# Three engines put on a written order of issue, from the output projection to the end of the first feed-forward loop

## The chip, the core and the metric

The kernel runs on one NeuronCore of one Trainium2 chip. The core has a matrix engine (TensorE, PE in the profile), a vector engine (VectorE, DVE), a scalar engine (ScalarE, ACT), GpSimd (POOL) and SyncE (SP), which here issues loads. Each of these works through its own instruction stream in order, and they wait for one another by semaphores. Tiles lie in SBUF (128 partitions); the sums of TensorE go to PSUM, which has eight banks of 128 x 512 floats. The metric is the device time of one execution in microseconds: 1062.6 us for the kernel before, the median of three runs (1062.28 to 1067.63).

## What is computed

One transformer-like block on 512 tokens of width 1024, all in float32, depth 1. Cut to what matters:

```python
h = rms_norm(x, mix_pre_g)
proj = h @ w_in                                   # convolution branch, state-space branch, gates
mixed = (g_conv * conv_out + g_ssm * ssm_out) @ w_out
x = x + rms_norm(mixed, mix_post_g)
h = rms_norm(x, ffn_pre_g)
gt, up = jnp.split(h @ w_gate_up, 2, axis=-1)     # hidden width 2816
f = (jax.nn.silu(gt) * up) @ w_down
x = x + rms_norm(f, ffn_post_g)
```

The change lies between `@ w_out` and the end of `h @ w_gate_up`. What stands before and after it in the program is not edited.

## The kernel before

**Precision.** Every float32 product is made of three faster ones: each operand is split into a rounded part (`...h`, `hi`) and the remainder (`...l`, `lo`), and `mm3` (lines 182 to 186) issues high x high, low x high and high x low into one PSUM sum. So every weight piece of 128 x 1024 has to be split: a copy on ScalarE (line 140 or 860) makes the high part, a subtraction on VectorE (line 145 or 863) the low part.

**Loads.** `w_raw` (line 133) loads the pieces on SyncE's queue, in the order of the program, into five buffers called `raw`. A buffer is loaded again when the last reader of what it held is done. Pieces 105 to 112 are the eight of W_out, 113 to 116 the first of each of the feed-forward slices 0 to 3, 117 to 120 the second of each of these, 121 and on the rest.

**Output projection (lines 1039 to 1057 and 1088 to 1126).** The 512 tokens are four tiles `t` of 128; each has two sums `tm_wo_t_n` of 512 columns, so eight banks, with eight steps `k` of contraction: 24 matmuls for each sum, `wo_step`. As soon as a token tile is summed, `residual(t)` makes of it the new residual stream: squares on ScalarE (`jk_a`), the product with the gain on VectorE (`mg`), a factor by GpSimd (`pm_a`, `rs_a`), the sum with x (`xr`), again squares (`jk_b`) and a factor (`pm_b`, `rs_b`), and a diagonal matrix `dg` of that factor. `turned(t)` multiplies by this diagonal on TensorE, which transposes and normalises at once (`ptr`), `gained` multiplies by the gain (`xg`: one half on VectorE, one on ScalarE).

**Feed forward, first product (lines 1059 to 1308).** It is done by a seven-product scheme (Winograd's form of Strassen's) for each of 22 slices `u` of weights. The moving operands are seven forms of the normalised tokens: `b11`, `b21`, `b22`, `t1` to `t4`; the first half of each comes from token tiles 0 and 1, the second from tiles 2 and 3, so most are complete only when all four tiles are through (`late_forms(3)`). The weight forms are `a11/a12` (from the first piece), `s1`, `s3/a22` and `s2/s4` (four additions of 128 x 512 on VectorE, line 888, then three splits). The products go to two banks for each slice, `xy` and `v`: `x1`, `y1`, `x2`, `v1`, `x3`, `v2`, `x4`, of 12 matmuls each with 256 columns. Between them halves of the banks are copied out (ScalarE, lines 1196, 1205, 1213) or added out (VectorE, line 1184): `x2` may not write into its bank before `x1_out` and `y1_out` have read it. The copies go to tiles `sg` and `f32`, whose memory lies where the pools of the residual and the late forms lay (closed in lines 1173 and 1174).

**What sets the order.** The Tile framework schedules the traced program at compile time with its own costs, and each engine's stream is the result. `pin(last, engines)` (line 171) takes the instructions of an engine after `last` in the order of the program and adds an edge from each to the next. Such an edge is an order within one stream, and no semaphore. In the kernel before, lines 1058 to 1167 (from `square_a(1, 0)` to `first(4)`) are pinned on the three engines, and so is the loop of slices 5 to 21 (lines 1278 to 1308); the first part (lines 1039 to 1057) and the loop of slices 0 to 4 (lines 1169 to 1277) are left to the scheduler.

Of the kernel before, what the change touches and what calls it, by code (L numbers as in the profile page):

```python
# [17 lines left out]
PE_Q, ACT_Q, DVE_Q = [getattr(mybir.EngineType, n) for n in ("PE", "Activation", "DVE")]  # L18
# [89 lines left out]
ORDER += [(_b, _j) for _b in BLOCKS for _j in range(NQ)]  # L108


def b3(ap, n):

    return ap.unsqueeze(len(ap.shape)).to_broadcast(list(ap.shape) + [n])
# [3 lines left out]
def block_kernel(ctx: ExitStack, tc: tile.TileContext, x, xT, prm, hp, gp, w, out):  # L117
    nc = tc.nc
# [28 lines left out]
    def w_split(n, pool_=None, tags=None, bufs=2, parts=1):  # L147
        if n in split or n >= W_END:
            return
        for r in range(n, n + RAW_AHEAD):  # L150
            w_raw(r)
        tags, bufs = (tags, bufs) if tags else (("whi", "wlo"), W_BUFS)
        split[n] = [(pool_ or wp).tile([P, 1024], F32R, tag=tg, bufs=bufs, name=f"{tg}_{n}") for tg in tags]
        if parts == 1:
            w_part(n, slice(0, 1024))
# [15 lines left out]
    def pin(last, *engines):  # L171

        traced = nc.cur_bb.bb.instructions
        at = next(n for n in reversed(range(len(traced))) if traced[n] is last)
        edge = mybir.DependencyInfo(mybir.DependencyClass.NoSync, mybir.DependencyReason.DATA)
        for e in engines:
            row = [i for i in traced[at + 1 :] if i.engine == e]
            for one, two in zip(row, row[1:]):
                tc.add_manual_dep(two, one.name, edge, reason="order")
        return traced[-1]  # L180
# [272 lines left out]
    for j in range(NK):  # L453
# [11 lines left out]
        if j == 0:  # L465
# [7 lines left out]
            first = pv, pg  # L473
# [54 lines left out]
    def s1(g):  # L528
# [5 lines left out]
        for c2 in range(2):  # L534
            ps = aux_tile(f"pxT{g}_{c2}")
            for c in range(2):
                tok = slice((2 * c2 + c) * P, (2 * c2 + c + 1) * P)
                for e in range(2):
                    pe.transpose(ps[:, c * GW + e * P : c * GW + (e + 1) * P], s[f"x{e}"][:, tok], ident)
            cs = slice(2 * c2, 2 * c2 + 2)  # L540
            pv = ps.rearrange("p (c h d) -> p c h d", c=2, h=HG)
            dve.tensor_tensor(out=xdt[:, cs], in0=pv, in1=b3(dtt[:, cs, hs], HD), op=ALU.mult)
            dve.tensor_tensor(
                out=y[:, cs], in0=pv,
                in1=b3(hp_t[:, 2:3, hs].to_broadcast([P, 2, HG]), HD), op=ALU.mult,
            )
        dve.tensor_tensor(out=xdec, in0=xdt[:, : NT - 1], in1=b3(dec[:, : NT - 1, hs], HD), op=ALU.mult)
        ps = yd_tile(0, f"pBT{g}")
        for c in range(NT - 1):
# [329 lines left out]
    def steps_s(u):  # L879

        if u >= NF or (u, "s1") in forms:
            return [], [], [], [], []
        ra, rb_ = g_raw(u, 0), g_raw(u, 1)
        (a11, a12), (a21, a22) = [(r[:, :T], r[:, T:]) for r in (ra, rb_)]
        s1_ = w2.tile([P, T], F32, tag="s1", bufs=2, name=f"s1_{u}")

        def total(out_, one, two):
            return lambda: dve.tensor_tensor(out=out_, in0=one, in1=two, op=ALU.add)  # L888

        return (  # L890
            [total(s1_, a21, a22), total(a21, a11, a21)],
            [total(a11, s1_, a11), total(a12, a11, a12)],
            halve(("s1",), u, s1_, [w2.tile([P, T], F32R, tag=tg, bufs=2, name=f"{tg}_{u}") for tg in ("dhi", "dlo")]),
            halve(("s3", "a22"), u, rb_, pair_of_tiles()),
            halve(("s2", "s4"), u, ra, pair_of_tiles()),
        )
# [125 lines left out]
    def late_forms(t):  # L1022
# [13 lines left out]
            ("t1", t1, 1.0), ("t2", t2, -1.0), ("t3", t1, 1.0), ("t4", t2, 1.0), ("b22", x1, 1.0))}  # L1036
        return s, {n: v[0] for n, v in h.items()}, {n: v[1] for n, v in h.items()}

    for k in range(2, NK):
        w_split(wo0 + k, *((wp, ("whi", "wlo")) if k > 5 else (w2, ("chi", "clo"))), W_BUFS if k > 5 else 3)  # L1040
    ps = tm_tiles("wo")
# [15 lines left out]
    here = nc.cur_bb.bb.instructions[-1]  # L1057
# [14 lines left out]
    def first(u):  # L1072
        x1(u)
        y1(u)
# [70 lines left out]
    one, two, s1, s3, s2 = steps_s(0)  # L1145
# [19 lines left out]
    hi["t3"]()  # L1165
    lo["t3"]()
    first(4)
    pin(here, PE_Q, ACT_Q, DVE_Q)
    s["t4"]()
    for n in ("b22", "t4"):  # L1170
        hi[n]()
# [105 lines left out]
    here = nc.cur_bb.bb.instructions[-1]  # L1277
    for u in range(EARLY_U + 1, NF):
# [7 lines left out]
        one, two, s1, s3, s2 = steps_s(u + 1)  # L1286
# [73 lines left out]
    def f_form(n):  # L1360
        p, j = jobs[n]
        q = j // 2
        if (p, q) in f_forms:
            return
        if p == "d":
            hi, lo = [t.rearrange("p (k t) -> p k t", k=2) for t in f_room(n)]
            src, sign = f32[:, 2 * q : 2 * q + 2, :], 1.0
        else:
            hi, lo = [t.rearrange("p (k t) -> p k t", k=4) for t in f_room(n)]
            ka, kb = slice(4 * q, 4 * q + 4), slice(NPAIR + 4 * q, NPAIR + 4 * q + 4)  # L1370
            a11, a12, a21, a22 = f32[:, ka, c1], f32[:, kb, c1], f32[:, ka, c2], f32[:, kb, c2]
            s = room["s"][:, ka] if room else None
            if p == "p5":
                dve.tensor_tensor(out=s, in0=a22, in1=a21, op=ALU.subtract)
            elif p == "p6":
                dve.tensor_tensor(out=a21, in0=a11, in1=a21, op=ALU.add)
                dve.tensor_tensor(out=s, in0=a21, in1=a22, op=ALU.subtract)
            elif p == "p3":
                dve.tensor_tensor(out=s, in0=a12, in1=s, op=ALU.subtract)
            src = {"p1": a11, "p5": s, "p6": s, "p3": s, "p7": a21, "p2": a12, "p4": a22}[p]  # L1380
            sign = -1.0 if p in ("p1", "p7") else 1.0
        f_forms[p, q] = hi, lo
        act.activation(hi, src, AF.Copy, scale=sign)
        if sign > 0:
            dve.tensor_tensor(out=lo, in0=src, in1=hi.bitcast(F32), op=ALU.subtract)
        else:
            dve.scalar_tensor_tensor(out=lo, in0=src, scalar=-1.0, in1=hi.bitcast(F32), op0=ALU.mult, op1=ALU.subtract)

    here = pin(here, PE_Q, ACT_Q, DVE_Q)
    f_form(0)  # L1390
    for j in range(2):
        w_form(j)
# [5 lines left out]
    x4(NF - 1)  # L1398
    last_out(NF - 1)
    pin(here, PE_Q)  # L1400
    h2.close()
    pf = ctx.enter_context(tc.tile_pool(name="pf", bufs=1))
# [70 lines left out]
    for t in range(NT):  # L1473
        i, r = t % 2, t // 2
# [99 lines left out]
```

## Time and profile before

| what | value |
|---|---|
| median of three runs | 1062.6 us |
| the profiled execution, its own time | 1061.24 us |
| its span, first to last instruction | 1059.5 us |
| TensorE busy | 1040.6 us (98%) |
| VectorE busy | 826.2 us (78%) |
| ScalarE busy | 599.0 us (57%) |
| GpSimd busy | 93.4 us (9%) |
| mean granted TensorE clock | 0.994 |

A row of the view of stretches gives for each engine the microseconds busy in the stretch and, in brackets, how many instructions began in it; then the granted clock of TensorE (1.00 is full) and the DMA engines' share. A row of the timeline gives the start, the duration, the engine, the line, the operation, output and inputs, and in square brackets how long the engine had been idle and what released it. Matmuls overlap in that view: their cost is the distance from start to start. A row of the view of waits says who waited for whom: microseconds in total, times, the longest.

### The profile page before, as it was taken

To read this page: it belongs to the slowest core of one execution; us is meant where nothing else is said; L and a number is where in the kernel's file an instruction comes from. 1 tells how busy PE (TensorE), PEld (TensorE's weight loads), DVE (VectorE), ACT (ScalarE), POOL (GpSimd) and SP (SyncE) were. 2 spreads that over 40 slices of the span, in tenths; PEclk is the share of its full clock that TensorE was granted. 3 is DMA by queue.
4 is the path that set the end of the run, shared out by engine and by line. 5 is a ranking of instruction groups with operands and counts; after the bars stand their busy time and mean duration, and the time that the engine had idled before them with its cause. 6 is when DMAs were issued, how large, how long until landed. Compare 5 with 4: busy or idle time off the path is not lost.

```text
span 1059.5 us, 15639 instructions
## 1 busy us (share of the span) xinstructions
PE 1040.6 (98%) x6145; PEld 920.5 (87%) x6145; DVE 826.2 (78%) x1178; ACT 599.0 (57%) x970; POOL 93.4 (9%) x117
## 2 busy tenths in 40 slices
PE   8999999999999999999999999998999999999997
PEld 7888789888989898989888888888999999998886
DVE  7799897886589769787996545458998898879765
ACT  6657847594849373933332593266555555555641
POOL 2002001111101020100000100011000000022001
PEclk9999999999999999999999999999899999999999
DMA  7477563656544645362123313524443334168912
GB/s 278 131 182 218 141 142 96 179 127 167 125 125 111 182 105 154 103 156 61 60 80 123 97 45 134 179 83 117 134 125 121 120 101 162 58 122 182 296 37 80
DMA packets 39098, 138.75 MB, mean 131 GB/s; under 512 B 4592, under 2 KB 4848, under 8 KB 38000
## 3 DMA queue, kind: packets, MB, share of 16 engines
q1 hardware_dynamic: 27168, 93.12, 26.8%
q0 software_dynamic: 8352, 33.56, 15.9%
q10 hardware_dynamic: 3504, 11.08, 2.9%
q8 instruction: 48, 0.79, 0.3%
q14 instruction: 26, 0.21, 0.1%
HBM read 133.48 MB, written 4.26 MB: 130 GB/s over the span
## 4 chain that ended last, share of the span: by engine, by line
PE 78%; DVE 12%; ACT 6%; issue 2%; DMA 1%; POOL 0%; SPq 0%; DVEq 0%; POOLq 0%; ACTq 0%
DVE a L417 4%; PE xy L184 3%; PE xy L185 3%; PE xy L186 3%; PE yd L579 3%; PE pso L184 2%; PE pso L185 2%; PE v L184 2%; PE pso L186 2%; PE v L185 2%; PE v L186 2%; PE px L184 2%; PE px L185 2%; PE px L186 2%; PE sx L186 2%
## 5 line engine op out<-in xcount | busy, mean ns | idle before, releaser
L140 ACT CAST whi<-raw 128x1024 fp32r<-128x1024 f32 (+1 forms) x118 | 120.9, 1033 | 223.4 <-PE pC L185 43.4
L417 DVE SCALAR_TENSOR_TENSOR a<-v,prm_t,a 128x485 f32<-128x485 f32 (+17 forms) x240 | 179.7, 753 | 4.5 <-ACT a L414 0.9
L145 DVE TENSOR_TENSOR wlo<-raw,whi 128x1024 fp32r<-128x1024 f32 (+1 forms) x84 | 99.8, 1195 | 43.8 <-ACT whi L140 43.6
L184 PE MATMUL pz<-whi,hhi 128*128 128x256 f32 (+1 forms) x256 | 74.2, 290 | 0.0
L185 PE MATMUL pz<-wlo,hhi 128*128 128x256 f32 (+1 forms) x256 | 73.2, 286 | 0.0
L186 PE MATMUL pz<-whi,hlo 128*128 128x256 f32 (+1 forms) x256 | 72.8, 284 | 0.0
L143 POOL DMA_DIRECT2D wlo<-in_w x34 | 30.3, 891 | 257.3 <-ACT wlo L142 169.4
L184 PE MATMUL pso<-yh,whi 128*128 128x512 f32 x128 | 50.0, 393 | 0.0
L184 PE MATMUL px<-hhi,whi 128*128 128x512 f32 x128 | 49.9, 390 | 0.0
L185 PE MATMUL px<-hlo,whi 128*128 128x512 f32 x128 | 49.9, 390 | 0.0
L185 PE MATMUL pso<-yl,whi 128*128 128x512 f32 x128 | 49.9, 391 | 0.0
L186 PE MATMUL px<-hhi,wlo 128*128 128x512 f32 x128 | 49.8, 389 | 0.0
L186 PE MATMUL pso<-yh,wlo 128*128 128x512 f32 x128 | 49.8, 392 | 0.0
L185 PEld LDWEIGHTS pz<-wlo,hhi 128*128 128x128 f32 x256 | 49.0, 191 | 0.3
L184 PEld LDWEIGHTS pz<-whi,hhi 128*128 128x128 f32 x256 | 49.0, 191 | 0.2
L186 PEld LDWEIGHTS pz<-whi,hlo 128*128 128x128 f32 x256 | 49.0, 191 | 0.1
L863 DVE TENSOR_TENSOR wlo_g<-raw,whi_g 128x1024 fp32r<-128x1024 f32 x39 | 47.4, 1220 | 1.7 <-ACT whi_g L860 1.2
L860 ACT CAST whi_g<-raw 128x1024 fp32r<-128x1024 f32 x39 | 40.8, 1053 | 13.2 <-DVE raw L888 13.2
L400 ACT ACTIVATE L<-L,nacs 128x128 f32<-128x128 f32 x128 | 41.3, 392 | 1.9 <-POOL L L394 1.6
L494 DVE SCALAR_TENSOR_TENSOR x<-px,prm_t,x 128x511 f32<-128x511 f32 (+2 forms) x48 | 35.6, 743 | 1.5 <-ACT x L492 1.3
L142 ACT ACTIVATE wlo<-whi 128x1024 fp32r<-128x1024 f32 x34 | 35.9, 1056 | 0.2
L860 ACT CAST chi_g<-raw 128x1024 fp32r<-128x1024 f32 x24 | 25.1, 1055 | 13.3 <-DVE raw L888 11.1
(531 smaller groups left out, 3359.6 us busy)
## 6 DMA issues: line engine op xcount, KB each, us to landing
raw<-in_w SPq DMA_DIRECT2D x161, 512.0 KB, 3.7
wlo<-in_w POOLq DMA_DIRECT2D x34, 512.0 KB, 6.0
L<-scr POOLq DMA_DIRECT2D x8, 1024.0 KB, 5.4
raw_p<-in_w ACTq DMA_DIRECT2D x8, 512.0 KB, 7.8
chain<-in_w POOLq DMA_DIRECT2D x6, 512.0 KB, 6.2
xT<-in_xT SPq DMA_DIRECT2D x8, 256.0 KB, 5.5
xr<-in_x ACTq DMA_DIRECT2D x4, 512.0 KB, 5.4
x2d<-xr ACTq DMA_DIRECT2D x4, 512.0 KB, 2.8
```

The lines of the kernel that those rows point to most:

```text
L140: act.copy(hi[:, c], src[:, c])
L142: act.activation(lo[:, c], hi[:, c].bitcast(F32), AF.Copy, scale=-1.0)
L145: dve.tensor_tensor(out=lo[:, c], in0=src[:, c], in1=hi[:, c].bitcast(F32), op=ALU.subtract)
L184: mark["pe"] = pe.matmul(ps, lh, rh, start=start, stop=False, skip_group_check=more)
L185: pe.matmul(ps, lh, rl, start=False, stop=False, skip_group_check=more)
L186: pe.matmul(ps, ll, rh, start=False, stop=stop, skip_group_check=more)
L400: act.activation(L[:, h, c, :], L[:, h, c, :], AF.Exp, bias=nacs[:, c, HG * g + h : HG * g + h + 1])
L417: return dve.scalar_tensor_tensor(out=va[j][:, d:], in0=vs[j][:, : T - d], scalar=col("dw_w", j * KC + KC - 1 - d), in1=va[j][:, d:], op0= ...
L494: dve.scalar_tensor_tensor(out=a[:, d:], in0=ps[:, : T - d], scalar=col("ssm_w", i * KS + KS - 1 - d), in1=a[:, d:], op0=ALU.mult, op1=ALU ...
L579: pe.matmul(yd[c // 2][:, c % 2, h, :], s["L"][:, h, c, :], s["xdt"][:, c, h, :], start=True, stop=True)
L860: act.copy(hi, src)
L863: dve.tensor_tensor(out=lo, in0=src, in1=hi.bitcast(F32), op=ALU.subtract)
```

## The change

A table `ISSUE` gives, for TensorE, ScalarE and VectorE, a list of numbers. Number n is the n-th instruction (from 0) of that engine in program order, counted from the first instruction after `before_wo`, which is set just before line 1039, the splits of W_out's pieces. `listed` takes the engine's instructions from there to line 1389, puts them in the order of the list, and adds an edge from each to the next, as `pin` does. Both calls of `pin` for this part go; the last `pin(here, PE_Q)` of line 1400 stays and starts where the list ends. No instruction is added, dropped or altered, DMA issues on ScalarE's queue included (they are numbered like the others). SyncE and GpSimd get no list.

The lists have 2036 numbers for TensorE, 248 for ScalarE and 327 for VectorE. From 815, 128 and 154 on they are the order of the program, which is that of `pin` before; ahead of these they are a new order. Some of the numbers, counted out by the code:

- TensorE: 0 to 95 `tm_wo` of token tiles 0 and 2, 108-115 `ptr0`, 140-147 `ptr2`, 196-203 `ptr1`, 160-195 and 204-215 `tm_wo` of tile 3, 216-239 slice 0's `x1` and `y1`, 288-295 `ptr3`, 344-355 slice 0's `x2`, 356-367, 416-427 and 476-487 `v1` of slices 0, 1 and 2, 404-415 slice 1's `x2`, 536-547 `v1` of slice 3.
- VectorE: 51 to 54 the four additions of slice 0, 61 `dlo` (the low part of `s1`) of slice 0, 59 `clo_g11` and 64 `wlo_g10` (the low parts of slice 0's `s2/s4` and `s3/a22`), 33 and 48 the low parts of `a11/a12` of slices 2 and 3, 31 `dg1`, 49 `dg3`, 62 `t1l`, 68 and 65 `t4l` and `t3l` of token tiles 2 and 3, 73 `clo_g13`, 93 `dlo` of slice 3, 116 `wlo_g22`.
- ScalarE: 64 `dhi` of slice 0, 58 `chi_g11`, 66 `whi_g10`, 73 the first copy out of `xy`, 81 the last read of slice 0's `xy`.

```diff
--- before.py
+++ after.py
@@ -108,6 +108,28 @@
 ORDER += [(_b, _j) for _b in BLOCKS for _j in range(NQ)]
 
 
+ISSUE = (
+    (PE_Q,
+     "0-75 78-80 84-86 90-92 76-77 81-83 87-89 93-95 99-101 105-107 119-121 125-127 108-115 96-98 102-104 116-118 "
+     "122-124 128-130 134-136 148-150 154-156 131-133 137-139 151-153 157-159 140-143 184-195 160-171 144-147 196-203 "
+     "172-183 204-215 264-275 296-307 216-239 308-319 276-295 320-331 240-263 356-367 332-343 416-427 476-487 344-355 "
+     "380-391 404-415 368-379 440-451 428-439 392-403 464-475 500-511 452-463 536-547 488-499 524-535 512-523 548-559 "
+     "596-607 584-595 560-571 620-643 608-619 572-583 656-667 644-655 704-715 692-703 668-691 716-739 752-775 800-811 "
+     "740-751 776-787 812-814 788-799 815-2035 "),
+    (ACT_Q,
+     "0-3 5 4 11 6-9 12 10 13-14 64 16-18 15 29 19-20 22 30 21 31-35 41 49 58 37 66 42 36 38 43 27 44-46 39-40 48 50 "
+     "23-26 28 71 53-56 51 57 52 47 59-62 68 65 70 63 77 69 67 73 97 88 72 82 75 90 84 74 76 78 83 79 86 92 85 89 81 "
+     "87 104 93 98 80 91 99-100 94 103 95 105 108 96 101 106-107 102 109 112 110-111 114 118 116 119 117 115 120-121 "
+     "123 125 122 113 127 124 126 128-247 "),
+    (DVE_Q,
+     "0-4 6-7 5 8-9 51-52 10 13 12 11 14 16 15 21 17 61 19 25 18 20 26-29 53 22 30 54 31 33 48 59 34 64 35 23 36-37 32 "
+     "69 40-41 39 42 44 24 45 70 74 47 43 46 49 71 50 38 56 55 57 72 58 62 78 60 67 66 63 83 68 65 79 76 80 109 81 86 "
+     "73 75 82 84 99 88 77 89 87 85 101 90 102 91 103 93 106 95 92 96 104 123 100 94 107 112 108 105 111 113 98 110 "
+     "114 97 119 115 118 125 131 116 126 124 127 120 128 117 135 129 136 130 121 132 134 138 122 137 133 142 139 144 "
+     "140 143 148-149 145 151 150 146 153 152 147 141 154-326 "),
+)
+
+
 def b3(ap, n):
 
     return ap.unsqueeze(len(ap.shape)).to_broadcast(list(ap.shape) + [n])
@@ -175,6 +197,19 @@
         edge = mybir.DependencyInfo(mybir.DependencyClass.NoSync, mybir.DependencyReason.DATA)
         for e in engines:
             row = [i for i in traced[at + 1 :] if i.engine == e]
+            for one, two in zip(row, row[1:]):
+                tc.add_manual_dep(two, one.name, edge, reason="order")
+        return traced[-1]
+
+    def listed(first, table):
+
+        traced = nc.cur_bb.bb.instructions
+        at = next((n for n, i in enumerate(traced) if i is first), -1)
+        edge = mybir.DependencyInfo(mybir.DependencyClass.NoSync, mybir.DependencyReason.DATA)
+        for e, text in table:
+            row = [i for i in traced[at + 1 :] if i.engine == e]
+            turns = [r.split("-") for r in text.split()]
+            row = [row[n] for r in turns for n in range(int(r[0]), int(r[-1]) + 1)]
             for one, two in zip(row, row[1:]):
                 tc.add_manual_dep(two, one.name, edge, reason="order")
         return traced[-1]
@@ -1036,6 +1071,7 @@
             ("t1", t1, 1.0), ("t2", t2, -1.0), ("t3", t1, 1.0), ("t4", t2, 1.0), ("b22", x1, 1.0))}
         return s, {n: v[0] for n, v in h.items()}, {n: v[1] for n, v in h.items()}
 
+    before_wo = nc.cur_bb.bb.instructions[-1]
     for k in range(2, NK):
         w_split(wo0 + k, *((wp, ("whi", "wlo")) if k > 5 else (w2, ("chi", "clo"))), W_BUFS if k > 5 else 3)
     ps = tm_tiles("wo")
@@ -1165,7 +1201,6 @@
     hi["t3"]()
     lo["t3"]()
     first(4)
-    pin(here, PE_Q, ACT_Q, DVE_Q)
     s["t4"]()
     for n in ("b22", "t4"):
         hi[n]()
@@ -1386,7 +1421,7 @@
         else:
             dve.scalar_tensor_tensor(out=lo, in0=src, scalar=-1.0, in1=hi.bitcast(F32), op0=ALU.mult, op1=ALU.subtract)
 
-    here = pin(here, PE_Q, ACT_Q, DVE_Q)
+    here = listed(before_wo, ISSUE)
     f_form(0)
     for j in range(2):
         w_form(j)
```

## The prediction

> **What bounds the kernel now.** I read the page first, then the waits of TensorE over the whole run, then stretches around them. On the page TensorE is busy for 98% of the span, so whatever can be won is what TensorE loses, and it loses in two ways: it stands, or it runs at a lower clock.
>
> ```profile
> span 1059.5 us, 15639 instructions
> ```
>
> The view of TensorE's waits has these five rows from the part that is changed; the view cut to 860 to 1060 us has none at all.
>
> ```profile
> PE v L184 <- ACT sg L1213: 3.4, 1, 3.4
> PE xy L184 <- ACT sg L1205: 1.0, 1, 1.0
> PE v L185 <- DVE t1l L1007: 0.9, 1, 0.9
> PE xy L184 <- DVE sg L1184: 0.5, 1, 0.5
> PE v L184 <- ACT t1h L1003: 0.5, 1, 0.5
> ```
>
> They sum to 6.3 us. The stretches show where they lie and what they cost beside themselves.
>
> ```profile
> core 0: us, PE busy (x) PEld busy (x) DVE busy (x) ACT busy (x) POOL busy (x), PEclk, DMA share, GB/s
> 670.00:721.12 51.12, 51.12 (x252) 43.22 (x250) 26.77 (x43) 26.25 (x57) 5.07 (x8) 1.00 0.48 153
> 721.12:736.99 15.87, 15.87 (x137) 15.68 (x135) 14.43 (x23) 9.38 (x20) 1.95 (x2) 1.00 0.21 72
> 736.99:743.61 6.62, 1.91 (x13) 1.51 (x12) 6.62 (x11) 3.33 (x7) 0.00 (x0) 0.91 0.43 140
> 743.61:749.32 5.71, 5.71 (x27) 5.71 (x28) 4.57 (x9) 3.18 (x8) 0.00 (x0) 0.50 0.05 22
> 749.32:779.00 29.68, 29.67 (x255) 29.44 (x255) 28.51 (x44) 19.01 (x30) 0.00 (x0) 1.00 0.47 149
> 779.00:790.00 11.00, 9.46 (x79) 8.93 (x78) 10.86 (x18) 6.10 (x12) 0.00 (x0) 1.00 0.46 140
> 790.00:850.00 60.00, 60.00 (x532) 60.00 (x531) 52.59 (x80) 32.49 (x54) 0.00 (x0) 1.00 0.36 113
> ```
>
> Until 721 TensorE is full and VectorE stands for 51.12 - 26.77 = 24.4 us. From 721 to 790 it is the other way about: VectorE is busy for 65.0 of 68.9 us, and TensorE waits. After the pause before 743.61 the granted clock is 0.50 for 5.71 us. From 790 on TensorE never stands.
>
> Now the loss as one number. These rows of TensorE's timeline give its pace and the two pauses.
>
> ```profile
> 672.20 0.39 PE L184 MATMUL tm_wo<-whi,m0h 128*128 128x512 f32 x1
> 674.92 0.39 PE L184 MATMUL tm_wo<-whi,m0h 128*128 128x512 f32 x1
> ...
> 721.12 0.28 PE L184 MATMUL xy<-b11h,a01h 128*128 128x256 f32 x1
> ...
> 729.60 1.95 PE L983 MATMUL ptr<-dg,xr 128*128 128x128 f32 x16
> 731.30 0.37 PE L184 MATMUL xy<-b11h,whi_g 128*128 128x256 f32 x1
> ...
> 737.50 0.38 PE L184 MATMUL v<-t1h,dhi 128*128 128x256 f32 x1 [0.51 <-ACT t1h L1003]
> 738.74 0.38 PE L185 MATMUL v<-t1l,dhi 128*128 128x256 f32 x1 [0.85 <-DVE t1l L1007]
> 738.96 0.28 PE L186 MATMUL v<-t1h,dlo 128*128 128x256 f32 x1
> ...
> 739.98 0.28 PE L186 MATMUL v<-t1h,dlo 128*128 128x256 f32 x1
> 743.61 0.58 PE L184 MATMUL v<-b22h,chi_g 128*128 128x256 f32 x1 [3.35 <-ACT sg L1213]
> ```
>
> From 738.96 to 739.98 nine matmuls of 256 columns start: 0.1133 us each. The 72 between 721.12 and 729.60 took 0.1178 each, a `ptr` of one token tile 1.70 (729.60 to 731.30), and one of 512 columns 2.72 / 12 = 0.227. Between 721.12 and 790.00 the table counts 137 + 13 + 27 + 255 + 79 = 511 matmuls, 16 of them the `ptr`. At full pace they take 72 x 0.1178 + 423 x 0.1133 + 1.70 = 58.1 us; they took 68.9. **The loss is 10.8 us**: 6.2 of standing, 27 x (5.71 / 27 - 0.1133) = 2.65 at half clock, and 1.9 in slow first matmuls after waits.
>
> [...]
>
> **Why TensorE stands at 740.** The rows of the other two engines at that place, and those that give VectorE's pace:
>
> ```profile
> 713.77 0.29 DVE L958 TENSOR_SCALAR dg<-ident,rs_b 128x128 f32<-128x128 f32 x1 [0.74 <-POOL rs_b L812]
> ...
> 726.52 0.21 DVE L811 TENSOR_SCALAR pm_b<-ss_b,ss_b 128x1 f32<-128x1 f32 x1 [0.34 <-ACT jk_b L804]
> ...
> 737.40 0.69 DVE L863 TENSOR_TENSOR dlo<-s,dhi 128x512 fp32r<-128x512 f32 x1
> 738.00 0.69 DVE L1007 TENSOR_TENSOR t1l<-t,t1h 128x512 fp32r<-128x512 f32 x1
> ...
> 739.80 1.22 DVE L863 TENSOR_TENSOR wlo_g<-raw,whi_g 128x1024 fp32r<-128x1024 f32 x1
> 740.94 0.69 DVE L1007 TENSOR_TENSOR t3l<-t,t3h 128x512 fp32r<-128x512 f32 x1
> ...
> 742.15 0.69 DVE L1007 TENSOR_TENSOR t4l<-t,t4h 128x512 fp32r<-128x512 f32 x1
> ...
> 743.35 0.42 DVE L1184 TENSOR_TENSOR sg<-xy,sg 128x256 f32<-128x256 f32 x1
> 743.68 0.69 DVE L888 TENSOR_TENSOR raw<-raw,raw 128x512 f32<-128x512 f32 x1
> ```
>
> ```profile
> 732.93 1.05 ACT L860 CAST chi_g<-raw 128x1024 fp32r<-128x1024 f32 x1 [4.07 <-DVE raw L888]
> ...
> 742.91 0.37 ACT L1196 COPY sg<-xy 128x256 f32<-128x256 f32 x1 [2.35 <-DVE t4l L1007]
> 743.18 0.38 ACT L1213 COPY sg<-v 128x256 f32<-128x256 f32 x1
> ```
>
> The product that stands needs a copy out to `sg`; the first such copy waits for `t4l`, the last form of the closed pools, whose memory `sg` takes. So VectorE's queue up to `t4l` sets the end of the pause, and TensorE has nothing listed ahead of it.
>
> **The change, part by part.** No work is added or removed; every term is a time at which an engine arrives.
>
> TensorE, up to 721. The new order permutes 240 matmuls of W_out and three `ptr`. VectorE and ScalarE have idle time there, so I let TensorE end W_out at 721.1 as before; cost 0. If that cover fails, a late `dg` costs its own lateness. `ptr2` goes behind the last step of token tile 1, which thus ends 1.70 earlier, and with it `dg1`: 713.77 - 1.70 = 712.1 start, 712.4 end.
>
> TensorE, from 721. By its list: 72 matmuls (8.48), `ptr3` (1.70), then `xy4`'s `x1`, `xy1` (36 matmuls, 4.08), so `v1` of slice 0 begins at 735.4. Then `v1` of slices 0, 1 and 2 and the `y1` of slice 4 (48, 5.44) before the first product that needs a copy out, at 740.8. Before, only slice 0's `v1` stood there. Then `xy1`'s `x2` at 743.5, `v1` of slice 3 at 754.4 (eight groups of 12 on), `xy5`'s `x2` at 770.7 (twelve more).
>
> VectorE. Seven of slice 0's entries (places 10, 11, 21, 30, 33, 37, 39 of the new list) move into the idle time before 721: five of 128 x 512 at 0.60 (737.40 to 738.00) and two of 128 x 1024 at 1.14 (739.80 to 740.94), 5.3 us in all. Behind `dg1`, place 35 starts at 712.4. Sums of its places, with 0.33 for a 256-column addition (743.35 to 743.68), against TensorE's times above:
>
> Places 35 to 67 (`t1l`): 5 x 1.14 + 25 x 0.60 + 2 x 0.21 + 0.29 = 21.4, so 733.8 against 735.4. Places 68 to 75 (`t4l`, `t3l`): 8 x 0.60, so 738.6; with a copy of 0.37, an addition of 0.60 in the way and one of 0.42, 740.0 against 740.8. Places 76 to 82 (`clo_g13`): 3 x 0.60 + 3 x 0.33 + 1.14 = 3.9, so 742.5 against 743.5. Places 83 to 97 (`dlo` of slice 3): 3 x 1.14 + 4 x 0.33 + 8 x 0.60 = 9.5, so 752.0 against 754.4. Places 98 to 121 (`wlo_g22`): 7 x 1.14 + 9 x 0.33 + 8 x 0.60 = 15.8, so 767.8 against 770.7.
>
> VectorE is ahead each time, by 0.8 to 2.9 us. That is thin, as these sums assume it never stands for a semaphore; one that writes what the last one wrote is 0.1 slower (0.69 for 0.60), which over 41 entries eats some 0.9. So some stalls will come.
>
> Loads. Place 45 is the first that reads piece 118, which loads when piece 113's buffer is free, after place 37, at 712.4 + 3 x 1.14 = 715.8. The view of the tile `raw` from 670 to 800 us has the time from issue to landing:
>
> ```profile
> DMA to landing us min/median/max: 3.4/4.1/7.1
> ```
>
> With the median it is there at 719.9; place 45 comes at 712.4 + 4 x 1.14 + 6 x 0.60 = 720.6. With the longest landing VectorE is 2.3 late, which the slack above does not cover wholly.
>
> ScalarE has 9.38 of 15.87 us and 19.01 of 29.68 busy in the table, so its cost is nothing while its list and VectorE's agree on who waits for whom: its first copy to `sg` stands behind the same `t4l` and `t3l`, and if ScalarE is late, VectorE's `lo` parts are, one for one. Its DMA issues (`xr`, `x2d`, `raw4`) move with it; the new `xr` loads are issued some microseconds ahead of the sums that read them. SyncE's loads and GpSimd's factors keep their order and come earlier as buffers and sums do.
>
> Behind 790 nothing is edited in the order, and TensorE never waits there, so what is won by 790 is won at the end.
>
> The sum: 10.8 us of loss go; new stalls cost between 0 (the checkpoints hold) and 5.5 (VectorE is ahead by no more than the 5.3 us moved). I take 1.0, nearer the first, since five checkpoints hold and the thinnest is missed by 0.1 with the slower spacing. 1061.24 - 10.8 + 1.0 = 1051.4 for the profiled execution; the median shown lies 1.4 above that execution, so **1053 us**.
>
> **Rivals.** *VectorE stays the bound.* It is busy for 65.0 of 68.9 us from 721 to 790, and TensorE, freed of its pauses, runs into it again at 779. Then only the 5.3 us moved count: 1057.3. Against it: the sums, and 24.4 us of idle time that dense packing opens.
>
> *A buffer holds ScalarE.* Its place 33, `chi_g11`, needs one of three buffers with W_out's pieces 108 to 110. Piece 108 is read last by tile 3's step 3, which the new TensorE order ends at 712.8; if the buffer given is that of 109 or 110, ScalarE stands until 720.9, 8.1 us, with `b11h`, `xg1` and `t1h` behind it. TensorE then stands after W_out, drops to half clock, and is some 7.1 late (8.1 less the slack of about 1): 10.8 - 1.0 - 7.1 = 2.7 won, 1060. [...]
>
> *Slower: the part behind the list is planned otherwise.* The scheduler orders the down projection after what the list made of its clock.
>
> ```profile
> 950.00:1000.00 50.00, 50.00 (x222) 41.40 (x222) 41.86 (x39) 28.72 (x34) 7.84 (x9) 1.00 0.85 221
> 1000.00:1020.00 20.00, 20.00 (x90) 16.58 (x89) 18.98 (x21) 14.63 (x16) 0.00 (x0) 1.00 0.41 145
> ```
>
> VectorE is full there too. If each of its seven products waits for one split that now stands behind other work (ScalarE's cast 1.05 and VectorE's 1.14, 2.2 us), that is 15.3: 1053 + 15.3 = 1068. It decides from 9.8 / 7 = 1.4 us for each product. Against it: not one wait there today, and the same instructions in the same program order.
>
> That the change does not do what it says is out: an edge within an engine fixes its stream.
>
> **Chances.** Forecast 0.68, VectorE the bound 0.15, the held buffer 0.10, slower 0.07. A measurement of this kernel tells about 0.5% (5.3 us) from no change. The forecast and half of the first rival are faster by more than that: 0.74; the other half and the held buffer are the same: 0.19; slower 0.07. The range runs from 1061.24 - 10.8 = 1050.4 up to the held buffer's 1060.
>
> **What would show it.** Right: no wait of TensorE above 1 us between 721 and 800, clock 1.00 in every stretch, the first copy out of `xy` near 740 instead of 742.91, some 58 us for the 511 matmuls. Wrong: a pause at `ptr3` or at slice 0's first `x2` (VectorE late), ScalarE standing before a `chi_g` cast until W_out ends (the buffer), TensorE waits behind 860 us (the plan behind the list), or VectorE standing for a `raw` load.

## The result and the profile after

The changed kernel takes 1051.53 us, the median of four runs (1050.49 to 1052.29), against 1062.44 us for four of the kernel before (1059.29 to 1067.63). The ratio is 0.9886, with a 95% interval from 0.9851 to 0.992. By the ratio the time is 0.9886 x 1062.44 = 1050.3 us, where 1053 was forecast with a range from 1050.4: faster by about what was said, and by the ratio 0.1 us under the low end. The interval of the ratio stands for a gain of 8.5 to 15.8 us; the two medians lie 10.9 apart. The profiled execution took 1052.29 us.

The page of the changed kernel, its span and its busy times:

```profile
span 1050.5 us, 15636 instructions
...
PE 1035.7 (99%) x6145; PEld 916.9 (87%) x6145; DVE 823.1 (78%) x1178; ACT 598.5 (57%) x970; POOL 94.5 (9%) x117
```

The work is the same; the span is 9.0 us shorter. The view of TensorE's waits over the whole run keeps one row from the changed part (the columns are total, times, longest):

```profile
PE v L219 <- ACT sg L1271: 0.9, 1, 0.9
```

The five rows of before, 6.3 us, are gone; this one is new. The stretches of the changed kernel, cut at the same times as those of before:

```profile
core 0: us, PE busy (x) PEld busy (x) DVE busy (x) ACT busy (x) POOL busy (x), PEclk, DMA share, GB/s
670.00:721.12 51.12, 51.12 (x251) 43.24 (x250) 31.52 (x51) 26.98 (x54) 4.81 (x7) 1.00 0.45 147
721.12:736.99 15.87, 15.87 (x136) 15.71 (x135) 15.19 (x27) 11.38 (x26) 3.22 (x3) 1.00 0.53 158
736.99:743.61 6.62, 6.62 (x60) 6.62 (x60) 6.62 (x13) 4.76 (x13) 0.00 (x0) 1.00 0.00 0
743.61:749.32 5.71, 5.71 (x51) 5.71 (x50) 5.71 (x8) 3.71 (x5) 0.00 (x0) 1.00 0.62 202
749.32:779.00 29.68, 28.74 (x251) 28.54 (x250) 27.28 (x44) 17.12 (x29) 0.00 (x0) 1.00 0.42 140
779.00:790.00 11.00, 11.00 (x99) 11.00 (x98) 10.16 (x16) 5.81 (x11) 0.00 (x0) 1.00 0.38 124
790.00:850.00 60.00, 60.00 (x532) 60.00 (x531) 54.43 (x83) 33.08 (x56) 0.00 (x0) 1.00 0.39 119
```

The numbers in brackets count the instructions that run in a stretch, those that began before it included, and not only those that begin in it; a matmul that runs across a border stands in both rows. As one row each, the stretch from 721.12 to 790.00 reads so before and after:

```profile
721.12:790.00 68.88, 62.62 (x505) 61.26 (x504) 64.99 (x100) 41.00 (x74) 1.95 (x2) 0.95 0.37 118
```

```profile
721.12:790.00 68.88, 67.94 (x588) 67.58 (x587) 64.96 (x104) 42.77 (x81) 3.22 (x3) 1.00 0.41 133
```

Three things are to be seen. The granted clock is 1.00 in every stretch: no half clock is left. Between 721.12 and 790.00 TensorE runs 588 matmuls where it ran 505. And VectorE, which stood for 24.4 us before 721, now stands for 51.12 - 31.52 = 19.6: 4.75 us of its work have moved ahead. From 790 the stretch holds the same 532 matmuls as before.

TensorE's timeline of the changed kernel at the first matmul of W_out, the first of the feed forward, the one that still waits, and the last of the feed forward's first product:

```profile
672.96 0.39 PE L219 MATMUL tm_wo<-whi,m0h 128*128 128x512 f32 x1
...
721.88 0.28 PE L219 MATMUL xy<-b11h,whi_g 128*128 128x256 f32 x1
...
756.92 0.38 PE L219 MATMUL v<-t1h,dhi 128*128 128x256 f32 x1 [0.94 <-ACT sg L1271]
...
935.08 0.28 PE L221 MATMUL xy<-t4h,clo_g 128*128 128x256 f32 x1
```

The same last matmul in the kernel before:

```profile
944.04 0.28 PE L186 MATMUL xy<-t4h,clo_g 128*128 128x256 f32 x1
```

From first to last the product took 944.04 - 721.12 = 222.92 us and takes 935.08 - 721.88 = 213.20 now: **9.7 us won in this stretch**. W_out itself began 0.77 later in this execution (672.96 for 672.20), which the change doesn't touch; that is why the span fell by 9.0 only.

### The profile page after: what moved, and what is told of

It reads as the page before. It is cut to its first block, busy times and chain, and to the rows that moved or that the text cites. A ratio compares the mean times of both kernels' runs of the same rounds, so it can differ in the third digit from the quotient of the medians.

```text
span 1050.5 us, 15636 instructions
## 1 busy us (share of the span) xinstructions
PE 1035.7 (99%) x6145; PEld 916.9 (87%) x6145; DVE 823.1 (78%) x1178; ACT 598.5 (57%) x970; POOL 94.5 (9%) x117
## 4 chain that ended last, share of the span: by engine, by line
PE 81%; DVE 9%; ACT 6%; issue 2%; DMA 1%; POOL 0%; SPq 0%; DVEq 0%; POOLq 0%; ACTq 0%
DVE a L452 4%; PE xy L220 4%; PE xy L219 4%; PE xy L221 4%; PE yd L614 3%; PE pso L219 2%; PE pso L220 2%; PE pso L221 2%; PE v L219 2%; PE v L220 2%; PE v L221 2%; PE px L221 2%; PE px L220 2%; PE px L219 2%; PE sx L220 2%
```

## Experiments

The prediction's account is that the three lists work together: forms of slice 0 and parts of other slices are made in VectorE's idle time before 721, and three `v1` groups fill TensorE until the first copies out are through. I call it theory A; the expectations set against it the accounts that they name. The numbers in the lists are those of the change. Many of these kernels' times fall into two groups some 6 to 9 us apart, the kernel before and the changed one among them; the fifth part below tells what they are. Where a difference is taken within the quicker group, the text says so. The quicker group of the kernel before has its median at 1061.06, 1060.94 and 1061.07 us in the three larger sets of runs, so those sets can be compared.

### The change once more

> The changed kernel once more, to size the gain. Theory A (the gain is the 10.8 us that TensorE lost, less 0.94 of new standing): 9.7 us from the first W_out matmul to the last matmul, ratio 0.990 to 0.992. Rival (something else is won too, as the first ratio of 0.9886 says): 12 us, ratio 0.987 to 0.989.

Measured: 1050.95 us, median of 6 runs (1049.72 to 1059.68), against 1062.64 of 23; ratio 0.9897 (0.986 to 0.9935). Four runs lie between 1049.7 and 1051.5, two at 1057.8 and 1059.7. Within the quicker group it is 1050.24 against 1061.06: 10.8 us. The wait for ScalarE is there again (0.8 us).

### Which list does it

TensorE's list alone, VectorE and ScalarE pinned as before:

```diff
 ISSUE = (
     (PE_Q, ...),
-    (ACT_Q, ...),
-    (DVE_Q, ...),
 )
...
     first(4)
+    pin(here, ACT_Q, DVE_Q)
...
+    pin(here, ACT_Q, DVE_Q)
     here = listed(before_wo, ISSUE)
```

> TensorE by its list alone; VectorE and ScalarE pinned where they were before and left to the scheduler elsewhere. Theory A (the gain needs VectorE packed into its idle time): no more than half the gain, 1057 to 1066 us where the kernel before has 1062. Rival B (TensorE's order is what counts): 1052 to 1053.

Measured: 1070.11 us (1068.54 to 1071.61, 7 runs), ratio 1.007 (1.0041 to 1.0099): slower than the kernel before, outside what either account had for it. The three longest waits of its TensorE between 700 and 800 us:

```profile
PE xy L204 <- DVE wlo_g L881: 5.9, 2, 5.1
PE v L202 <- ACT dhi L878: 2.8, 1, 2.8
PE xy L202 <- ACT whi_g L878: 2.5, 1, 2.5
```

And its stretch up to 721.12:

```profile
670.00:721.12 51.12, 50.36 (x248) 42.20 (x246) 23.88 (x39) 24.87 (x54) 5.09 (x8) 1.00 0.43 145
```

VectorE's work before 721 is 23.88 us, less than the 26.77 of the kernel before: nothing moves into its idle time. TensorE asks for the `v1` groups and a split of W_gate_up at the new times and finds them unmade.

The other two lists, TensorE pinned as before:

```diff
 ISSUE = (
-    (PE_Q, ...),
     (ACT_Q, ...),
     (DVE_Q, ...),
 )
...
     first(4)
+    pin(here, PE_Q)
...
+    pin(here, PE_Q)
     here = listed(before_wo, ISSUE)
```

> VectorE and ScalarE by their lists; TensorE pinned where it was before and left to the scheduler elsewhere. Theory A: VectorE is as early as in the changed kernel but TensorE has nothing to do ahead of slice 0's x2, so a pause of 1 to 2 us stays there, and 5 to 8 us are won. Rival C (VectorE's order is all): 9 to 10 us.

Measured: 1063.17 us (1061.77 to 1071.72, 10 runs), ratio 1.0018 (0.9987 to 1.0049): nothing won, so theory A's number for it missed. The four longest of TensorE's seven waits between 700 and 800:

```profile
PE xy L203 <- ACT b21h L1022: 2.8, 1, 2.8
PE xy L204 <- DVE b21l L1026: 1.1, 1, 1.1
PE xy L204 <- DVE b11l L1026: 0.9, 1, 0.9
PE xy L203 <- DVE sg L1204: 0.7, 1, 0.7
```

The loss moved forward, to right behind W_out. TensorE's old order asks for `b21` after the 12 matmuls of slice 0's `x1`; the new list has 36 ahead of it (264-275, 296-307, 216-227), and VectorE and ScalarE are ordered for that. The gain belongs to neither half: each, without the other, loses all of it, and TensorE's list alone loses more.

All three lists as the order of the program:

```diff
-    (PE_Q, "0-75 78-80 84-86 ... 815-2035 "),
-    (ACT_Q, "0-3 5 4 11 ... 128-247 "),
-    (DVE_Q, "0-4 6-7 5 ... 154-326 "),
+    (PE_Q, "0-2035"),
+    (ACT_Q, "0-247"),
+    (DVE_Q, "0-326"),
```

> Three lists as in the changed kernel, each the plain order of the program. Theory A (which order is what counts): slower than the kernel before, 1070 us or more, since VectorE does each slice's preparation in one piece ahead of the additions that free a bank. Rival (being held to one order on three engines is what counts): 1052 to 1056.

Measured: 1111.13 us (1104.41 to 1113.22, 4 runs), ratio 1.043 (1.038 to 1.048). TensorE's waits:

```profile
PE xy L204 <- DVE sg L1204: 27.9, 3, 13.4
PE xy L204 <- DVE f L1204: 13.9, 2, 7.0
```

Being held to a list is worth nothing by itself; this one costs some 50 us against the 1061.28 of the kernel before beside it. The gain is in these numbers, in this order.

### The steps of the prediction, one by one

VectorE's and ScalarE's work on slice 0's weight forms, and on the first of slice 1's that need the same buffers, put back behind the residual of the last token tile (eleven entries of VectorE, four of ScalarE):

```diff
     (ACT_Q,
-     "... 13-14 64 16-18 ... 49 58 37 66 42 ... 23-26 28 71 53-56 51 57 52 47 ..."
+     "... 13-14 16-18 ... 49 37 42 ... 23-26 28 53-56 51 57 64 58 66 71 52 47 ..."
     (DVE_Q,
-     "... 8-9 51-52 10 ... 17 61 19 ... 43 46 49 71 50 38 ..."
+     "... 8-10 ... 17 19 ... 43 46 49-52 61 53-54 59 64 69-70 74 71 38 ..."
```

> The changed kernel with slice 0's weight forms, and the first of slice 1's that need their buffers, put back behind the residual of the last token tile: eleven entries of VectorE (7.7 us) and four of ScalarE. Theory A: VectorE reaches t3l 3 to 8 us later, TensorE stands before slice 0's v1 and x2, and 4 to 8 us of the gain are lost. Rival (there is slack for it): within 1 us of the changed kernel.

Measured: 1062.74 us (1061.33 to 1070.48, 10 runs), ratio 1.0001 (0.9972 to 1.0031). Within the quicker group that is 1062.61, so 12.4 us are lost, more than the moved work comes to (7.7 us). VectorE's work before 721.12 is 27.28 us there, near the 26.77 of the kernel before. One wait of TensorE holds most of it:

```profile
743.89 0.58 PE L204 MATMUL v<-t1h,dhi 128*128 128x256 f32 x1 [9.26 <-ACT t1h L1023]
```

Its cause stands on the other engines: VectorE, SyncE's first load behind 700 us, and ScalarE.

```profile
733.38 1.23 DVE L883 TENSOR_TENSOR clo_g<-raw,chi_g 128x1024 fp32r<-128x1024 f32 x1 [1.12 <-ACT chi_g L880]
...
738.10 0.69 DVE L908 TENSOR_TENSOR s<-raw 128x512 f32<-128x512 f32 x1 [2.36 <-DMA raw<-in_w]
```

```profile
734.63 1.46 SPq L143 DMA_DIRECT2D raw<-in_w  x2
```

```profile
738.83 0.62 ACT L880 CAST dhi<-s 128x512 fp32r<-128x512 f32 x1 [4.53 <-DVE s L908]
...
743.21 0.63 ACT L1023 ACTIVATE t1h<-t 128x512 fp32r<-128x512 f32 x1
```

`clo_g11`, the last reader of a `raw` buffer, ends at 734.61; at 734.63 SyncE issues the load into that buffer (in the changed kernel its first load here goes out at 716.83); VectorE stands for it until 738.10, ScalarE stands for VectorE until 738.83, and `t1h` is behind both. A late step is paid along this ring, and then again in pace: behind the 9.26 us the 24 matmuls from 745.41 to 750.53 start 0.213 us apart, as they do in the kernel before where the granted clock is 0.50 (25 from 743.99 to 749.32).

The two added `v1` groups put behind slice 0's `x2`, so that only slice 0's own stands there:

```diff
     (PE_Q,
-     "... 332-343 416-427 476-487 344-355 380-391 ..."
+     "... 332-343 344-355 416-427 476-487 380-391 ..."
```

> As the changed kernel, but TensorE's v1 of slices 1 and 2 (24 matmuls, 2.7 us) goes behind slice 0's first x2. Theory A (they are what TensorE does while t4l, t3l and the first copies are made): TensorE stands 2 to 2.7 us before that x2, and the time is 1.5 to 2.5 us longer than the changed kernel's. Rival (VectorE's packing alone is enough): no pause above 0.5 us, the same time within 0.5.

Measured: 1054.49 us (1051.89 to 1062.08, 10 runs), ratio 0.9927 (0.9897 to 0.9957). Within the quicker group 1053.68, so 3.4 us are lost. Its timeline of TensorE:

```profile
740.62 0.38 PE L204 MATMUL xy<-t2h,chi_g 128*128 128x256 f32 x1 [2.38 <-DVE sg L1204]
...
741.20 0.41 PE L205 MATMUL xy<-t2l,chi_g 128*128 128x256 f32 x1
...
744.60 0.29 PE L206 MATMUL v<-t1h,dlo 128*128 128x256 f32 x1
```

The pause is where the prediction put it and about as long as its sums say: 2.38 us where 24 matmuls of filler are 2.7. Behind it lies what I had not priced: the 16 matmuls from 741.20 to 744.60 take 3.40 us, 0.213 each, again the distance of the kernel before at a granted clock of 0.50, after a pause of only 2.4 us. That is 1.6 us beside the pause.

The first four steps of token tile 3's second sum (184 to 195) ordered behind `ptr1` and the last four steps of its first sum, so that a buffer with a piece of W_out comes free later:

```diff
     (PE_Q,
-     "... 140-143 184-195 160-171 144-147 196-203 172-183 204-215 ..."
+     "... 140-143 160-171 144-147 196-203 172-195 204-215 ..."
```

> The changed kernel with one edit on TensorE: the first four steps of tile 3's second sum go behind ptr1, so the buffer of W_out's piece 108 comes free 5 us later and ScalarE's chi_g11 with it. Theory A: ScalarE stands about 5 us there and the lists behind it are late by as much; TensorE loses 3 to 5 us. Rival (another buffer is free): no change within 0.5 us.

Measured: 1058.12 us (1056.73 to 1066.4, 10 runs), ratio 0.9982 (0.9953 to 1.001). Within the quicker group 1057.73, so 7.5 us are lost, close to the rival's 7.1 and above what I expected for this edit. Its timeline of ScalarE:

```profile
718.44 2.00 ACT L880 CAST whi_g<-raw 128x1024 fp32r<-128x1024 f32 x2 [7.22 <-PE tm_wo L206]
```

ScalarE stands for 7.22 us at a split whose buffer TensorE still reads (`whi_g`, not the `chi_g11` that prediction and expectation had named), and `b11h` is behind it. In the changed kernel the same row has a wait of 0.16 us, at 711.91: the order of twelve matmuls within W_out is what brings the held buffer. The 7.5 us are not the buffer's alone: TensorE also waits 1.4 us for `dg1`, since `ptr1` now stands twelve matmuls earlier. And the pace stays, where the rival had half clock: behind waits of TensorE of 1.36 and 1.11 us the 33 matmuls from 726.24 to 729.99 start 0.114 us apart, and the mean granted clock of the execution is 0.998, as in the changed kernel.

### The wait that is left

ScalarE's number 81, the last read of slice 0's bank, put right behind 79; then the same with 92 behind 85, and VectorE's 101 to 103, additions that read piece 122, behind 90, 91 and 93, which don't:

```diff
     (ACT_Q,
-     "... 83 79 86 92 85 89 81 87 ..."
+     "... 83 79 81 86 92 85 89 87 ..."
```

> As the changed kernel, but ScalarE's last read of slice 0's bank (number 81) stands ahead of the two dhi casts, not behind them. Theory A (the one pause left, 0.94 us, comes from a load that is 1.6 late and holds both VectorE and ScalarE): the pause shrinks to about 0.4, as dlo of slice 3 is late by the same load; 0.4 us shorter. Rival (only ScalarE's order holds TensorE): the pause goes, 0.9 us shorter.

```diff
     (ACT_Q,
-     "... 83 79 86 92 85 89 81 87 ..."
+     "... 83 79 81 86 85 92 89 87 ..."
     (DVE_Q,
-     "... 87 85 101 90 102 91 103 93 106 ..."
+     "... 87 85 90-91 93 101-103 106 ..."
```

> As e7_silu_early, and on VectorE the additions of slice 3 and its dlo go ahead of the additions of slice 4 that wait for the load; ScalarE's dhi of slice 4 goes behind a cast. Theory A: no pause is left, 0.9 us shorter than the changed kernel. Rival (the late load holds something else next): the pause only moves, the same time.

Measured: the first 1056.74 us (1051.1 to 1058.62, 10 runs), ratio 0.9928 (0.99 to 0.9956); the second 1053.92 us (1048.7 to 1059.35, 6 runs), ratio 0.9904 (0.9867 to 0.9941). TensorE has no wait left between 700 and 800 us in either, so on the pause of the first the rival was right. And yet neither median is better than the change's: of their runs eight in ten and three in six lie in the longer group, and the three quicker runs of the second have the median 1050.37, where the changed kernel's have 1050.24. The profiled execution of the second was the shortest seen of any kernel here, 1048.7 us:

```profile
719.98 0.28 PE L204 MATMUL xy<-b11h,whi_g 128*128 128x256 f32 x1
...
931.50 0.28 PE L206 MATMUL xy<-t4h,clo_g 128*128 128x256 f32 x1
```

931.50 - 719.98 = 211.52 us, 1.7 less than the change and 11.4 less than before. So the wait that is left and what comes with it are worth some 1.7 us between these two profiled executions; the times don't show it, as something else decides whether it is had.

### What the two groups are

The hundred microseconds from 800 to 900, where TensorE is always busy at a granted clock of 1.00, in three executions. The kernel before, in an execution of 1061.24 us:

```profile
800.00:900.00 100.00, 100.00 (x885) 100.00 (x884) 88.17 (x133) 53.66 (x89) 0.00 (x0) 1.00 0.38 122
```

The change without its filler, 1061.68 us, of the longer group:

```profile
800.00:900.00 100.00, 100.00 (x852) 100.00 (x851) 86.42 (x130) 52.56 (x89) 0.00 (x0) 1.00 0.38 125
```

The kernel with number 81 early, 1056.31 us, of the longer group:

```profile
800.00:900.00 100.00, 100.00 (x852) 100.00 (x851) 84.59 (x127) 51.28 (x86) 0.00 (x0) 1.00 0.38 123
```

Without those that had begun before 800, TensorE starts 882 matmuls or 849, one each 0.1133 us or 0.1178. These are the two distances that the prediction read off as 0.1133 and 0.1178 and took for two places in the program. They are two paces, and in these profiles TensorE kept one until a pause, a `ptr`, half clock or a late matmul broke the row: the last group of `ptr` was followed by the short one in every profile but that of TensorE's list alone, W_out by the long one wherever no wait came between, and behind a pause or a late matmul it was now the one, now the other. In the profile of the change, behind a distance of 0.18 us at 743.04, the long pace ran from 743.2 to 755.7, 106 matmuls or 0.48 us. How far the groups lie apart then hangs on how many matmuls follow the last break. In the kernel before 1,402 follow its last wait, from 785.1 to 944.0: 1402 x 0.0045 = 6.3 us, and its groups lie 5.9 to 6.4 apart in the three larger sets. In the change without its filler they are the 1,694 from 744.7 on: 7.6 us, and 8.1 measured. In the changed kernel they lie 8.5 apart, with two runs only in the longer group, where 1,570 matmuls give 7.1.

To hold the pace I added two plain float32 matmuls of the identity to the loop, which write into slice 8's bank and are overwritten by its first product. They are work that the computation doesn't need. Where there is a list, TensorE's then ends at 2037.

```diff
+        if u in (8,):
+            t0 = bank(f"xy{u}")
+            idle.insert(0, held.pop(f"xy{u}"))
+            for _ in range(2):
+                pe.matmul(t0[:, :P], ident, ident, start=True, stop=True)
         x1(u)
```

With the two moves above, in the kernel before, and in the changed kernel:

> As e8_both_moves, with two matmuls of ident by ident (plain float32, 128 columns) into the bank that slice 8's x1 then overwrites. Executions of one kernel fall in two groups some 6.6 us apart, and in the traces the 256-column matmuls from about 775 to 945 us run at 113.3 ns from start to start in the shorter ones and at 117.8 in the longer; after every ptr block, of the same kind, the pace was 113.3. Theory P (the pace is set anew by such a block and then stays): no execution in the longer group, all at 1049 to 1052, at a cost of 0.5 us. Rival (the pace is chosen otherwise, at the start of the execution for instance): both groups stay.

> The kernel before with the same two matmuls ahead of slice 8's x1. Theory P: its longer group (1066 to 1068) goes too, all executions at 1059 to 1063, so the gain of the change is the same against it, 9 to 10 us. Rival: both groups stay.

> The changed kernel, its three lists as they are, with the two matmuls ahead of slice 8's x1, so that it stands against e11_before_lock at one pace. Theory A (the change wins what TensorE lost, 10.8 less 0.94 of new standing): all executions in one group, 9.5 to 10 us under e11_before_lock's 1062.15, so 1052.2 to 1052.7. Rival (the first ratio is right, 12 us): 1050.

Measured, all on one chip:

| kernel with the two matmuls | us, median | runs | lowest to highest | ratio (95%) |
|---|---|---|---|---|
| both moves | 1051.20 | 6 | 1049.91 to 1052.02 | 0.9887 (0.9859 to 0.9916) |
| before | 1062.15 | 12 | 1060.45 to 1063.45 | 0.999 (0.997 to 1.0009) |
| changed | 1052.34 | 6 | 1050.97 to 1053.36 | 0.9896 (0.9865 to 0.9928) |

None of the 24 runs is in the longer group, while 11 of the 27 runs of the unaltered kernel before beside them are. The first kernel's stretch has the short pace:

```profile
800.00:900.00 100.00, 100.00 (x885) 100.00 (x884) 88.34 (x133) 53.72 (x89) 0.00 (x0) 1.00 0.37 124
```

With the pace out of the comparison the change is worth 1062.15 - 1052.34 = **9.8 us**. The runs of the kernel before beside these two kernels differ by 0.6 in the quicker group (1061.07 and 1060.46), so 9.2 to 9.8. The kernel with both moves and the two matmuls is the one to keep: its median is that of the changed kernel (1051.53 and 1050.95 in its two sets), but none of its six runs lies above 1052.02, where the changed kernel reached 1059.68. The pace in the profiled executions of all three was already short where the two matmuls stand, so that they set it follows from the 24 runs and is not seen in a trace. No run put two matmuls of another kind there: whether it is their kind, or any change in the row at this place, isn't shown.

## Why the prediction was right, and where it was not

**What TensorE loses, and why: right.** The five waits and the half clock are gone, and most of the loss with them: by the timelines 9.7 us were won, within the quicker group 10.8, at one pace 9.2 to 9.8, where 9.8 were forecast.

**The size of the loss: wrong, and it is the step that failed.** "Between 721.12 and 790.00 the table counts 137 + 13 + 27 + 255 + 79 = 511 matmuls": this sum counts the matmuls that run across a border twice. The stretch as one row has 505, and the first of these is the last one of W_out, so 504 began there. At full pace they take 72 x 0.1178 + 416 x 0.1133 + 1.70 = 57.3 us, not 58.1, and the loss is 68.9 - 57.3 = 11.6 us, not 10.8. The whole product says the same. It is 22 slices of 84 matmuls and 16 of `ptr`; at full pace it would take 8.48 + 1775 x 0.1133 + 1.70 = 211.3 us from first to last start, and took 222.92. The kernel without a wait took 211.52, 11.4 less than before. The low end, "1061.24 - 10.8 = 1050.4", took the short count for the most that can be won; with 11.6 it is 1049.6, below the 1050.3 of the ratio.

Nor did the range leave room for the two paces, though one of the three runs shown, 1067.63, lay apart. The ratio says 12.1 us, more than any loss explains: one of four runs of before lies in the longer group and none of the four of the change. Without that run the medians are 10.8 apart (1062.28 and 1051.53). The draw of four runs and the short count together put the result below the range; neither is the mechanism.

**The sum: close by luck.** 10.8 - 1.0 = 9.8 was forecast, and the timelines have 11.4 - 1.7 = 9.7. Both terms were too small, by about the same. Of the 1.7 us that the changed kernel still loses against the kernel without a wait, 0.94 is the wait and 0.48 the longer pace; the rest is not traced. (The chances, too, are summed loosely: 0.68 and half of 0.15 are 0.755, not 0.74.)

**TensorE up to 721: right.** The 240 permuted matmuls cost nothing; W_out ended at 721.88, 0.77 late for having begun 0.77 late.

**5.3 us moved ahead of 721: nearly.** 4.75 by the stretches, 5.1 if the stretch is shifted by the 0.77. That the gain needs the early work is shown by the kernel that takes it back, with slice 1's first forms: all of the gain is lost, though by way of a late load and not by the work's own length.

**The checkpoints: two of five held.** All times of the prediction shift by the 0.77. VectorE's timeline of the changed kernel at each (`t1l`, `t3l`, `clo_g13`, the load that it stood for, `dlo` of slice 3, `wlo_g22`):

```profile
734.78 0.69 DVE L1042 TENSOR_TENSOR t1l<-t,t1h 128x512 fp32r<-128x512 f32 x1
...
739.81 0.69 DVE L1042 TENSOR_TENSOR t3l<-t,t3h 128x512 fp32r<-128x512 f32 x1
...
743.21 1.22 DVE L898 TENSOR_TENSOR clo_g<-raw,chi_g 128x1024 fp32r<-128x1024 f32 x1
...
752.73 0.69 DVE L923 TENSOR_TENSOR s<-raw 128x512 f32<-128x512 f32 x1 [1.61 <-DMA raw<-in_w]
...
755.75 1.29 DVE L898 TENSOR_TENSOR dlo<-s,dhi 128x512 fp32r<-128x512 f32 x2
...
771.24 1.22 DVE L898 TENSOR_TENSOR wlo_g<-raw,whi_g 128x1024 fp32r<-128x1024 f32 x1
```

| entry | end by the prediction, + 0.77 | end measured | needed by TensorE, + 0.77 |
|---|---|---|---|
| `t1l` | 734.6 | 735.5 | 736.2 |
| `t3l` | 739.4 | 740.5 | 741.6, with the copies behind it |
| `clo_g13` | 743.3 | 744.4 | 744.3 |
| `dlo` of slice 3 | 752.8 | 756.4 | 755.2 |
| `wlo_g22` | 768.6 | 772.5 | 771.5 |

Ends are the start plus the duration, for the pair at 755.75 the first of the two. The sums were short by 0.9 to 1.1 at the first three, and the third, 0.1 behind by the table, made TensorE wait for nothing. The cause is not the slower spacing that the prediction had put at 0.9: between 713 and 757 us VectorE's TENSOR_TENSOR rows of 512 columns are followed by the next 0.60 us later, except where it stands. It is `dg1`, which began 0.2 later than forecast, short stands, the longest 0.44 for GpSimd's factor ahead of `dg3`, and 0.1 from taking the end as start plus duration. At the fourth VectorE was 3.6 later than forecast, 1.61 of it for a load and 0.66 for a bank that TensorE still wrote, and behind TensorE's time; the fifth it still missed by that table, but TensorE was by then itself 1.4 later (0.94 of waiting, 0.48 at the longer pace).

**The load: right in kind, wrong in place.** The late one was piece 122 at place 92, not piece 118 at place 45. Nor did VectorE itself hold TensorE there. ScalarE's timeline of the changed kernel shows how the load reached it:

```profile
753.46 0.62 ACT L895 CAST dhi<-s 128x512 fp32r<-128x512 f32 x1 [1.16 <-DVE s L923]
755.26 1.05 ACT L895 CAST whi_g<-raw 128x1024 fp32r<-128x1024 f32 x1 [1.18 <-DVE raw L923]
...
756.48 0.39 ACT L1271 ACTIVATE sg<-xy 128x256 f32<-128x256 f32 x1
```

ScalarE's last read of slice 0's bank stands behind two splits that wait for VectorE's additions, and slice 3's `v1` needs that bank; with 81 moved ahead, the wait is gone. I had let ScalarE's late entries delay VectorE's `lo` parts only, and not asked which of them frees a bank. So new standing came, as forecast, but by this other way.

**The first copy out near 740: right.** ScalarE's row:

```profile
740.53 0.37 ACT L1231 COPY sg<-xy 128x256 f32<-128x256 f32 x1 [1.17 <-DVE t3l L1042]
```

It stands for `t3l`, as said. Without the filler TensorE waits 2.38 us for what follows it.

**The rivals.** *VectorE stays the bound* is out: it is busy for 15.19 + 6.62 + 5.71 + 27.28 + 10.16 = 65.0 of 68.9 us as before, and TensorE hardly waits. Beside the same busy time 83 more matmuls run, because its work is in another order. *A buffer holds ScalarE* did not come, but one misplaced group of twelve brings it, near the price named: 7.22 us of standing and 7.5 on the clock, without half clock and with another wait in it. *The part behind the list* is planned no worse: from 860 us on TensorE of the changed kernel has no wait, and from the last matmul of this product to the end of the span it takes 1050.5 - 935.08 = 115.4 us, as before (1059.5 - 944.04 = 115.5).

**The clock.** The prediction put half clock behind the pause of 3.35 us and its length at 5.71. The kernel before, cut where the granted clock changes, shows both otherwise:

```profile
740.26:742.46 2.20, 0.00 (x0) 0.00 (x0) 2.20 (x4) 0.30 (x1) 0.00 (x0) 1.00 0.18 34
742.47:743.61 1.14, 0.00 (x0) 0.00 (x0) 1.14 (x3) 0.70 (x3) 0.00 (x0) 0.50 0.74 284
743.61:749.30 5.69, 5.69 (x26) 5.69 (x27) 4.55 (x9) 3.16 (x8) 0.00 (x0) 0.50 0.05 22
```

Half clock began 2.2 us into the pause and lasted 1.14 + 5.69 = 6.83 us. Without the filler the matmuls 0.213 us apart came after a pause of 2.38 us and took 3.40; the changed kernel's wait of 0.94 us left the granted clock at 1.00. What sets the start and the length was not shown.

## What to carry to other kernels

Put orders of several engines together as one: a list for one engine that presumes another's can cost more than having none, as TensorE's did here; the other two won nothing without it. When an order is checked by arithmetic, ask of each late entry not only who waits for what it writes, but also which bank or buffer it frees. Before a difference of some microseconds is explained, count the matmuls in a stretch where nothing waits: two executions of the changed kernel (1049.72 and 1059.68) differ by as much as the change won. And ask for the count of a long stretch as one row: summed over short ones, it counts what runs across their borders twice, which here hid 0.8 us of the loss.

## What the runs showed of the hardware that I had not expected

TensorE ran rows of 256-column matmuls, each with its weight load, at one of two exact distances, 0.1133 and 0.1178 us, at the same granted clock of 1.00, and kept a pace for up to 1,700 of them. Some 6 us of an execution of the kernel before hang on which it is, about two thirds of what the whole change is worth. A wait of 0.94 us changed it in the profile of the change. With two plain float32 matmuls in the row no run of 24 was in the longer group, at a price: beside the quicker group of their chip (1061.07 us) the kernel before with them took 1062.15, 1.1 us more, where 0.5 was expected. What in the hardware sets the pace stays open.

Without the filler TensorE stood for 2.38 us, and its matmuls slowed to 0.213 us only from 741.20 on, 0.6 after it had resumed at 740.62, and not at once; in the kernel before the granted clock fell to 0.50 within the pause, 2.2 us after its start.
